# Attention's steps at fixed visits in a one-core encoder trunk

## The chip, the cores and the metric

The kernel runs on one core of a Trainium2 chip. The metric is the device time of one execution in microseconds (us). Five engines work side by side, each from its own queue and in that queue's order: TensorE (PE, matmuls; its weight loads are shown apart as PEld), VectorE (DVE), ScalarE (ACT), GpSimd (POOL) and SyncE (SP, which here issues transfers). Transfers run on 16 DMA engines. One engine waits for another through semaphores.

## The reference, cut to what matters

A trunk of two layers over 256 tokens of width 1024, all float32. A layer has a token mixer and a gated MLP, each behind an RMSNorm and with a residual sum. The mixer, cut to its core:

```python
u, q, k, v, g_pool, g_attn = split(xn @ w_in)
pool_out = (window means of u, four widths, minus u) @ w_pool * pool_scale
for g, (window, dilation) in enumerate(((128, 1), (512, 4), (2048, 16))):
    logits = q_g @ k_g * scale + bias_g           # +-64 keys, strided by the dilation
    o_g = softmax(logits) @ v_g ; lse_g = logsumexp(logits)
attn = sum over g of softmax_over_groups(lse)_g * o_g     # 4 heads of 128
merged = sigmoid(g_pool) * (pool_out @ w_a) + sigmoid(g_attn) * (attn @ w_b)
h = h + merged @ w_o
```

The weighted sum over the three groups equals one softmax over the keys of all three groups together, and that is how the kernel computes it: for each of the four heads and each half of the tokens one row of 512 logits (256 for group 0, 128 each for groups 1 and 2), one exponential, one division, and one sum of products with v over all of them.

## The kernel before, in words

Tokens are kept as two interleaved halves t = 0, 1 of 128. Nearly all matrix products are made with operands split into a high and a low part ("wh" and "wl" of weights, "xh" and "xl" of activations), so each weight tile that comes from memory as "raw" is cast to wh by ACT (line 177) and the rest made as wl by DVE (line 178). The class Weights does this in a fixed order of pieces given by `use`, up to three pieces ahead of the product that needs one; a 1 MB load into one of three raw buffers stands behind two pieces as a rule (`cols`: 256 columns, two pieces of 128). The load itself is line 117, on SP's queue.

`proj` (line 491 and 493) makes 128 output columns from one piece: eight matmuls with wh for 512 columns of x, eight with wl for 256. This is called a projection below. In a layer the mixer goes:

- values v of all twelve heads (lines 588, 757), then the pooling branch u, eight projections, and its window sums on DVE;
- q and k in six pairs of heads, PAIRS, four projections each (two heads of q, two of k). In the second pair (m == 1) a quarter of the pool products stands ahead of each projection (`pool_out`, matmuls at 483 to 485);
- eight projections of the pool branch with w_a into pa (`add_up`, 513 and 514), eight of the first gate, and then groups of the second gate and of w_b on attention's output at2.

Attention has four steps for each of the four heads hh:

- `scores` (881 to 908): for each t, matmuls of q and k into one bank (886, 891), bias added (897), negative maximum (902), exponential with its sum on ACT (905), reciprocal (907), scaling by it (908). It needs the head hh of all three groups, so heads 0 and 1 can go after the third pair and heads 2 and 3 after the sixth.
- `turn` (912 to 921): DVE transposes the probabilities in blocks of 32 x 32 into "rows" (915, one buffer, which shares its place with the norm's gain), and `cross` moves the sixteen blocks of 32 partitions to where a full transpose has them: sixteen transfers of 32 KB from "rows" to "pt" (598), on SP's queue. pt has one buffer.
- `parts` (923 to 931): pt's columns of group 0 split into high (pth, ACT, 929) and low (ptl, DVE, 930).
- `weigh` (933 to 949): six matmuls with split values (939) and eight with plain ones (943), the sum kept split in at2 (948, 949).

Before the change these steps stand in one list, two heads at a time: scores a, scores b, turn a, parts a, weigh a, turn b, parts b, weigh b. `step` takes the next one behind a projection: behind the second, third and fourth of the pairs m = 3, 4 and 5 until eight are done, and behind each of the eight projections into pa. The program is written in this order, and a planner, which has its own durations for each instruction, takes it as priorities: each engine's queue is filled with the first instruction in program order that is ready in the plan. So in the plan a weighting can come in the middle of a later projection, and the order on each engine is fixed when the kernel runs. Waits that come out longer than planned hold up everything behind them on that engine.

Of the kernel before, what the change touches and what calls it, by code (L numbers as in the profile page):

```python
# [10 lines left out]
F32 = mybir.dt.float32  # L11
# [5 lines left out]
P = 128  # L17
# [15 lines left out]
C_Q, C_K, C_V, C_GP, C_GA = 1024, 1024 + AW, 1024 + 2 * AW, 1024 + 3 * AW, 2048 + 3 * AW  # L33
# [3 lines left out]
WARM = (5, 1, 2, 1)  # L37
PAIRS = (2, 4, 0, 1, 3, 5)
LAG = 6
ENTRY = 4  # L40
HALVES = (slice(0, 512), slice(512, D))
SEGMENTS = (HALVES, (slice(0, 512), slice(512, 768), slice(768, D)))
# [162 lines left out]
def encoder(ctx, tc, x, w_in, w_pool, pool_scale, w_a, w_b, w_o, norm1, norm2, w_up, conv_w,  # L205
# [4 lines left out]
    big = ctx.enter_context(tc.tile_pool(name="big", bufs=1))  # L210
    sm = ctx.enter_context(tc.tile_pool(name="small", bufs=2))
# [5 lines left out]
    W = Weights(tc, wpool, big)  # L217

    def cols(w, c0):

        src = w[:, c0 : c0 + 256].rearrange("(k p) c -> p k c", p=P)
        return W.add(
            src, (8, 256), [((lambda t, j=j: t[:, :, j * P : (j + 1) * P]), (8, P)) for j in (0, 1)]
        )
# [10 lines left out]
    for l in range(DEPTH):  # L235
        for g in range(NG):
            c0 = C_V + g * 512
            slots = (("m2", 0, 2), ("m2", 1, 2), ("ybig",), ("at2",)) if g == 0 else ()
            for j in range(2):
                tag = "k1" if l == 0 and g == 1 and j == 0 else None  # L240
                W.use(rows(w_in[l], j * 512, 4, c0, 512, tag), slots[2 * j : 2 * j + 2])
        if l == 0:
            W.n_scaled = len(W.pieces)
        for c in range(3, -1, -1):
            W.use(cols(w_in[l], c * 256))
        for n, c in enumerate(PAIRS):
            pool = ([], [])
            if n == 1:
                pool = W.add(
                    w_pool[l].rearrange("g (k p) c -> p (g k) c", p=P), (8, 256),  # L250
                    [((lambda t, j=j: t[:, 4 * j : 4 * j + 4, :]), (4, 256)) for j in range(2)],
                )
                pool = (pool[:1], pool[1:])
            W.use(pool[0] + cols(w_in[l], C_Q + c * 256))
            W.use(pool[1] + cols(w_in[l], C_K + c * 256))
        for c in range(4):
            W.use(cols(w_a[l], c * 256))
        for c in range(4):
            W.use(cols(w_in[l], C_GP + c * 256))
        for c in range(2):  # L260
            W.use(cols(w_in[l], C_GA + c * 512))
            W.use(cols(w_in[l], C_GA + c * 512 + 256))
            src = w_b[l][:, c * 512 : (c + 1) * 512].rearrange("(k p) c -> p k c", p=P)
            W.use(
                W.add(
                    src, (4, 512),
                    [((lambda t, j=j: t[:, :, j * 256 : (j + 1) * 256]), (4, 256)) for j in (0, 1)],
                )
            )
        for c in range(4):  # L270
            W.use(rows(w_o[l], c * 256))
        slots = (("v1",), ("ybig",), ("at2",))
        for j in range(2):
            W.use(rows(w_up[l], j * 512, 4, 0, 512), slots[2 * j : 2 * j + 2])
        for f in range(0, NF, 2):
            a = cols(w_up[l], f * P) if f >= ENTRY else []
            g = cols(w_up[l], DFF + f * P)
            W.use([a[0], g[0], a[1], g[1]] if a else g)
            if f >= LAG:
                W.use(rows(w_down[l], (f - LAG) * P))  # L280
        for f in range(NF - LAG, NF, 2):
            W.use(rows(w_down[l], f * P))
# [5 lines left out]
    def gain(src):  # L288
        g = sm.tile([P, D], F32, tag="gain", bufs=1, name="gain")
        nc.sync.dma_start(out=g, in_=src.partition_broadcast(P))  # L290
        return g
# [203 lines left out]
    def proj(x2):  # L495

        i, (wh, wl) = W.get()
        ps = mmp.tile([P, 2, S], F32, tag="mm", name="proj_ps")
        two_sums(ps, lambda k: wh[:, k, :], lambda k: wl[:, k, :], x2, KD)
        W.free(i)  # L500
        return ps[:, 0], ps[:, 1]

    def halves(a):

        return a.rearrange("p (t m) -> p t m", t=2)
# [87 lines left out]
    def cross(out, in_):  # L593

        for i in range(4):
            for j in range(4):
                a, b = slice(32 * i, 32 * i + 32), slice(32 * j, 32 * j + 32)
                nc.sync.dma_start(out=out[b, i], in_=in_[a, j])  # L598

    def two_parts(tag, name):  # L600

# [163 lines left out]
    for l in range(DEPTH):  # L765
# [21 lines left out]
        if l == 0:  # L787
            with tc.manual_schedule():
                begun = begin_values_of_x()
            x2 = first_values(*begun, keep_values)  # L790
# [23 lines left out]
        for gi in range(3, -1, -1):  # L814
# [8 lines left out]
            cur, n = u, S + 2 * PAD  # L823
# [52 lines left out]
        q = big.tile([P, NH - HPG, 2, P], F32, tag="q1", name="q")  # L876
        kk = big.tile([P, NH - HPG, 2, P], F32, tag="k1", name="k")
        at2 = big.tile([P, HPG, 2, 2, P], F32R, tag="at2", name="at2")
        probs, ptiles = {}, {}

        def scores(hh):
            probs[hh] = sm.tile([P, 2, 512], F32, tag="s", name="probs")
# [29 lines left out]
        def turn(hh):  # L912

            rows = sm.tile([P, 4, 2, 4, 32], F32, tag="gain", bufs=1, name="rows")
            nc.vector.transpose(
                out=rows.rearrange("p j t c r -> p (t c) j r"),
                in_=probs[hh].rearrange("p t (c j r) -> p (t c) j r", c=4, j=4),
            )
            pt = sm.tile([P, 4, 2, 4, 32], F32, tag="pt", bufs=1, name="pt")
            cross(pt, rows)  # L920
            ptiles[hh] = pt

        def parts(hh):
            pt = ptiles[hh].rearrange("p i t c r -> p c t i r")
# [23 lines left out]
            nc.scalar.copy(out=oh, in_=ps)  # L948
            nc.vector.tensor_sub(out=ol, in0=ps, in1=oh.bitcast(F32))

        steps = []
        for a, b in ((0, 1), (2, 3)):
            steps += [(scores, a), (scores, b), (turn, a), (parts, a), (weigh, a)]
            steps += [(turn, b), (parts, b), (weigh, b)]

        def step():
            if steps:
                f, *which = steps.pop(0)
                f(*which)


        for m, c in enumerate(PAIRS):
            if m == 1:
                po2 = two_parts("m2", "po2")
                pool_parts = pool_out(po2)
            if m == 2:

                qkl = big.tile([P, 2, HPG, 2, P], F32R, tag="xn", name="qkl")
                ql, kl = qkl[:, 0], qkl[:, 1]
            for n in range(4):  # L970
                if m == 1:
                    next(pool_parts)
                src, rest = (halves(a) for a in proj(x2))
                hd = 2 * c + n % 2
                scale = HD**-0.5 if n < 2 else 1.0
                if hd < HPG:
                    hi, lo = ((qh, ql) if n < 2 else (kh, kl))
                    nc.scalar.mul(out=hi[:, hd], in_=src, mul=scale)
                    nc.vector.scalar_tensor_tensor(
                        out=lo[:, hd], in0=src, scalar=scale, in1=hi[:, hd].bitcast(F32),  # L980
                        op0=ALU.mult, op1=ALU.subtract,
                    )
                    nc.vector.scalar_tensor_tensor(
                        out=lo[:, hd], in0=rest, scalar=scale, in1=lo[:, hd].bitcast(F32),
                        op0=ALU.mult, op1=ALU.add,
                    )
                else:
                    o = (q if n < 2 else kk)[:, hd - HPG]
                    nc.scalar.mul(out=o, in_=rest, mul=scale)
                    nc.vector.scalar_tensor_tensor(  # L990
                        out=o, in0=src, scalar=scale, in1=o, op0=ALU.mult, op1=ALU.add
                    )
                if m >= 3 and n and len(steps) > 8:
                    step()

        pa = big.tile([P, KD, S], F32, tag="ybig", name="pa")
        for c in range(KD):
            add_up(pa[:, c, :], proj(po2))
            step()
        assert not steps  # L1000
        g2 = gain(norm2[l])


        gates = big.tile([P, 4, S], F32, tag="gates", name="gates")
# [7 lines left out]
        for c in range(KD):  # L1012
            th = gate(c)
            nc.vector.scalar_tensor_tensor(
                out=pa[:, c, :], in0=th, scalar=1.0, in1=pa[:, c, :], op0=ALU.add, op1=ALU.mult
            )
        m2 = big.tile([P, 2, KD, 2, P], F32R, tag="m2", name="m2")
        mh, ml = m2[:, 0], m2[:, 1]
        for c4 in range(2):
            ths = [gate(4 * c4 + j) for j in range(4)]  # L1020
            for j2 in range(2):
                i, (wh, wl) = W.get()
                for j in range(2):
                    c = 4 * c4 + 2 * j2 + j
# [3 lines left out]
                    m = sm.tile([P, S], F32, tag="u", name="m")  # L1028
# [5 lines left out]
                    m = halves(m)  # L1034
# [4 lines left out]
        x2 = two_parts("x", "x2")  # L1039
# [26 lines left out]

        a_first = big.tile([P, ENTRY, S], F32, tag="gates", name="a_first")

        rows_of_a = big.tile([P, 2, ENTRY * P], F32, tag="m2", name="a_rows")

# [5 lines left out]
        def turn_entry(t, r):  # L1076
            pt = mmp.tile([P, ENTRY, P], F32, tag="mm", name="a_turn")
            for f in range(ENTRY):
                nc.tensor.transpose(pt[:, f, :], r[:, f * P : (f + 1) * P], ident)
# [70 lines left out]
        for f in range(0, NF, 2):  # L1150
            up(f)
            up(f + 1)
            if f >= LAG:
                next(down)
                next(down)
        if l + 1 < DEPTH:
            x2 = two_parts("x", "x2")
# [34 lines left out]
```

## Time and profile before

| | us |
|---|---|
| median of 3 runs | 887.76 |
| the runs | 885.21, 887.76, 887.93 |
| profiled execution | 886.05 |
| its span, first to last instruction | 884.3 |
| PE busy in the span | 868.0 |
| DVE busy | 682.5 |
| ACT busy | 518.7 |

The granted clock of TensorE was 0.998 over the span. The page of the profile gives busy times, a chain of waits followed back from the last instruction, and the costliest groups. Views of the trace behind it answer more: the waits (who waited for whom), the timeline (instructions in order of time; neighbours of one kind merged, with "x16" for sixteen), and tables of busy time by stretch. In layer 0 attention's steps run from about 106 to 191 us, in layer 1 from about 544 to 626 us. A merged line of SP for `cross` gives the time that SP's queue took to issue the sixteen transfers.

### The profile page before, as it was taken

How to read it: one execution, taken by the hardware profiler on the slowest of the kernel's cores; microseconds unless marked ns; L12 is line 12 of the kernel's file. 1: busy time of each engine (PE TensorE's matmuls, PEld its weight loads, DVE VectorE, ACT ScalarE, POOL GpSimd, SP SyncE). 2: the span in 40 equal slices, each digit the busy share in tenths (PEclk: the TensorE clock that was granted, in tenths of full speed). 3: DMA queues.
4: the chain of work that ended last, by engine and by line, in shares of the span. 5: the costliest groups of instructions: out<-in, count | busy, mean ns of one | idle time of the engine just before them, and what ended most of it. 6: DMA issues, size and time to landing. Idle time of an engine off the chain costs nothing.

```text
span 884.3 us, 12920 instructions
## 1 busy us (share of the span) xinstructions
PE 868.0 (98%) x4778; PEld 752.8 (85%) x4778; DVE 682.5 (77%) x1150; ACT 518.7 (59%) x905; POOL 14.7 (2%) x45
## 2 busy tenths in 40 slices
PE   9999999999999999999999999999999999999997
PEld 7888887888888888888888898888888888888886
DVE  6997785857869987787756977776678698878774
ACT  6755553556648766666545564554566486656653
POOL 2000000000000000000000000000000000000000
PEclk9999999999999999999999999999999999999999
DMA  9669636466564665565626465544755447556541
GB/s 326 214 232 297 226 117 196 157 222 208 179 207 146 208 219 191 165 215 191 238 96 237 144 215 168 170 164 135 269 188 191 158 155 247 182 191 199 182 143 49
DMA packets 132236, 168.86 MB, mean 191 GB/s; under 512 B 5302, under 2 KB 112518, under 8 KB 132044
## 3 DMA queue, kind: packets, MB, share of 16 engines
q1 hardware_dynamic: 132156, 168.02, 57.0%
q8 instruction: 38, 0.62, 0.3%
q14 instruction: 26, 0.21, 0.1%
q10 hardware_dynamic: 16, 0.00, 0.0%
HBM read 162.74 MB, written 3.69 MB: 188 GB/s over the span
## 4 chain that ended last, share of the span: by engine, by line
PE 82%; SPq 8%; DMA 3%; DVE 3%; issue 1%; ACT 1%; ACTq 0%; POOLq 0%; POOL 0%; DVEq 0%
PE proj_ps L491 30%; PE proj_ps L493 16%; SPq L598 8%; PE res_ps L518 6%; PE v_ps L588 6%; PE res_ps L519 6%; PE res_ps L520 6%; PE v_ps L757 2%; PE b_ps L491 2%; DMA pt<-rows 2%; PE v_ps L670 1%; DMA raw<-in_w_in_dram 1%; PE o_ps L939 1%; PE o_ps L943 1%; PE b_ps L493 1%
## 5 line engine op out<-in xcount | busy, mean ns | idle before, releaser
L178 DVE TENSOR_TENSOR wl<-raw,wh 128x1024 fp32r<-128x1024 f32 x274 | 333.8, 1223 | 121.5 <-ACT wh L177 119.6
L177 ACT CAST wh<-raw 128x1024 fp32r<-128x1024 f32 x274 | 286.1, 1049 | 183.0 <-PE proj_ps L491 113.6
L491 PE MATMUL proj_ps<-x,wh 128*128 128x512 f32 x1408 | 353.2, 392 | 0.0
L491 PEld LDWEIGHTS proj_ps<-x,wh 128*128 128x128 f32 x1408 | 254.1, 189 | 46.0
L493 PEld LDWEIGHTS proj_ps<-x,wl 128*128 128x128 f32 x1408 | 192.5, 190 | 13.8
L493 PE MATMUL proj_ps<-x,wl 128*128 128x256 f32 x1408 | 197.6, 282 | 0.0
L518 PE MATMUL res_ps<-wh,actq 128*128 128x512 f32 (+1 forms) x184 | 70.2, 381 | 0.0
L519 PE MATMUL res_ps<-wl,actq 128*128 128x512 f32 (+1 forms) x184 | 70.1, 381 | 0.0
L520 PE MATMUL res_ps<-wh,actk 128*128 128x512 f32 (+1 forms) x184 | 69.9, 380 | 0.0
L520 PEld LDWEIGHTS res_ps<-wh,actk 128*128 128x128 f32 x184 | 34.6, 188 | 6.7
L518 PEld LDWEIGHTS res_ps<-wh,actq 128*128 128x128 f32 x184 | 34.7, 188 | 6.2
L519 PEld LDWEIGHTS res_ps<-wl,actq 128*128 128x128 f32 x184 | 34.7, 188 | 6.0
L491 PE MATMUL proj_ps<-po,wh 128*128 128x512 f32 x128 | 33.6, 396 | 0.0
L1122 ACT ACTIVATE y<-y 128x256 f32<-128x256 f32 x44 | 18.3, 416 | 24.4 <-DVE y L1119 24.2
L1105 ACT ACTIVATE y<-a,prm 128x256 f32<-128x256 f32 x36 | 21.6, 599 | 16.1 <-DVE a L514 16.1
L425 ACT ACTIVATE junk<-h 128x512 f32<-128x512 f32 (+1 forms) x20 | 10.9, 547 | 27.7 <-DVE h L423 27.7
L518 PE MATMUL res_ps<-wh,m 128*128 128x512 f32 (+1 forms) x72 | 26.5, 368 | 0.0
L519 PE MATMUL res_ps<-wl,m 128*128 128x512 f32 (+1 forms) x72 | 26.3, 366 | 0.0
L520 PE MATMUL res_ps<-wh,m 128*128 128x512 f32 (+1 forms) x72 | 26.3, 365 | 0.0
L491 PEld LDWEIGHTS proj_ps<-po,wh 128*128 128x128 f32 x128 | 22.7, 189 | 3.7
L588 PE MATMUL v_ps<-wh,x 128*128 128x512 f32 x80 | 25.7, 392 | 0.0
L1106 DVE SCALAR_TENSOR_TENSOR y<-a,prm,y 128x255 f32<-128x255 f32 x36 | 17.3, 481 | 8.1 <-ACT y L1105 8.1
(205 smaller groups left out, 1094.6 us busy)
## 6 DMA issues: line engine op xcount, KB each, us to landing
raw<-in_w_in_dram SPq DMA_DIRECT2D x58, 1024.0 KB
raw<-in_w_up_dram SPq DMA_DIRECT2D x44, 1024.0 KB
raw<-in_w_down_dram SPq DMA_DIRECT2D x22, 1024.0 KB
raw<-in_w_a_dram SPq DMA_DIRECT2D x8, 1024.0 KB
raw<-in_w_o_dram SPq DMA_DIRECT2D x8, 1024.0 KB
pt<-rows SPq DMA_DIRECT2D x128, 32.0 KB
raw<-in_w_b_dram SPq DMA_DIRECT2D x4, 1024.0 KB
sk<-fd SPq DMA_DIRECT2D x1, 2560.0 KB
```

Source lines behind the costliest of these rows:

```text
L177: lambda: nc.scalar.copy(out=h, in_=src),
L178: lambda: nc.vector.tensor_sub(out=l, in0=src, in1=h.bitcast(F32)),
L491: nc.tensor.matmul(ps, wh(k), x2[:, k], start=(k == 0), stop=False)
L493: nc.tensor.matmul(ps[:, 1], wl(k), x2[:, k, 0], start=False, stop=(k == nk - 1))
L518: nc.tensor.matmul(ps, ah, wh, start=first, stop=False)
L519: nc.tensor.matmul(ps, ah, wl, start=False, stop=False)
L520: nc.tensor.matmul(ps, al, wh, start=False, stop=last)
L588: nc.tensor.matmul(ps, x2[:, 2 * n + j, part, t, :], w[:, j, :], start=(n + m == 0), stop=(n == 3 and m == 5),)
L598: nc.sync.dma_start(out=out[b, i], in_=in_[a, j])
L757: nc.tensor.matmul(ps[t], a[:, k, t, :], w[:, j, :], start=(k + m == 0), stop=(k == KD - 1 and m == 2),)
L1105: nc.scalar.activation(y, a, AF.Identity, bias=b, scale=w1)
L1122: nc.scalar.activation(y2, y2, AF.Tanh, scale=c)
```

## The change

The places behind which a step can go are now called visits and counted from 0 to 27: the four projections of each pair m = 3, 4, 5 (0 to 11), the eight into pa (12 to 19) and the eight of the first gate (20 to 27). A table gives each step of each head its visit. Heads 0 and 1: scores at 0 and 3, turn at 1 and 5, parts at 6 and 10, weigh at 7 and 11. Heads 2 and 3: scores at 12 and 13, turn at 13 and 17, parts at 18 and 22, weigh at 19 and 23. `cross` becomes a generator that issues four transfers and pauses; each visit, after its steps, lets the oldest unfinished one go on. So a head's transfers stand in the program at four visits, from its turn's visit on for heads 0 and 2, and from the one after for heads 1 and 3, since the visit of their turn ends the one before.

pt is now one tile for two heads, in the place "ybig" for heads 0 and 1 (between plh, the pooled branch, and pa) and in the place "xn" for heads 2 and 3 (after qkl, the low parts of q and k). "rows" keeps its one buffer. Therefore the load of the second norm's gain, which has the same place as "rows", moves from before the gates to after the first gate. In the second pair each quarter of the pool products stands behind its projection and not ahead of it, and the pool weights' pieces stand between the two pieces of a column block.

```diff
+VISITS = ((0, 3, 12, 13), (1, 5, 13, 17), (6, 10, 18, 22), (7, 11, 19, 23))
...
-            W.use(pool[0] + cols(w_in[l], C_Q + c * 256))
-            W.use(pool[1] + cols(w_in[l], C_K + c * 256))
+            for j, c0 in enumerate((C_Q, C_K)):
+                a, b = cols(w_in[l], c0 + c * 256)
+                W.use([a] + pool[j] + [b])
...
             for j in range(4):
                 a, b = slice(32 * i, 32 * i + 32), slice(32 * j, 32 * j + 32)
                 nc.sync.dma_start(out=out[b, i], in_=in_[a, j])
+            yield
...
-        probs, ptiles = {}, {}
+        probs, ptiles, crossing = {}, {}, []
...
-            pt = sm.tile([P, 4, 2, 4, 32], F32, tag="pt", bufs=1, name="pt")
-            cross(pt, rows)
-            ptiles[hh] = pt
+            if hh % 2 == 0:
+                ptiles["pair"] = big.tile(
+                    [P, 2, 4, 2, 4, 32], F32, tag=("ybig", "xn")[hh // 2], name="pt"
+                )
+            ptiles[hh] = ptiles["pair"][:, hh % 2]
+            crossing.append(cross(ptiles[hh], rows))
...
-        steps = []
-        for a, b in ((0, 1), (2, 3)):
-            steps += [(scores, a), (scores, b), (turn, a), (parts, a), (weigh, a)]
-            steps += [(turn, b), (parts, b), (weigh, b)]
+        visits = [[] for _ in range(28)]
+        for f, at in zip((scores, turn, parts, weigh), VISITS):
+            for hh, visit in enumerate(at):
+                visits[visit].append((f, hh))
 
         def step():
-            if steps:
-                f, *which = steps.pop(0)
-                f(*which)
+            for f, hh in visits.pop(0):
+                f(hh)
+            if crossing and next(crossing[0], "end") == "end":
+                crossing.pop(0)
...
             for n in range(4):
+                src, rest = (halves(a) for a in proj(x2))
                 if m == 1:
                     next(pool_parts)
-                src, rest = (halves(a) for a in proj(x2))
...
-                if m >= 3 and n and len(steps) > 8:
+                if m >= 3:
                     step()
...
-        assert not steps
-        g2 = gain(norm2[l])
...
             nc.vector.scalar_tensor_tensor(
                 out=pa[:, c, :], in0=th, scalar=1.0, in1=pa[:, c, :], op0=ALU.add, op1=ALU.mult
             )
+            step()
+        assert not any(visits) and not crossing
+        g2 = gain(norm2[l])
```

## The prediction

> **What bounds the kernel now.** I read the page first, then the waits, then a table by stretch for the two stretches in which attention's steps run, then the timeline there. The page:
>
> ```profile
> span 884.3 us, 12920 instructions
> PE 868.0 (98%) x4778; PEld 752.8 (85%) x4778; DVE 682.5 (77%) x1150; ACT 518.7 (59%) x905; POOL 14.7 (2%) x45
> PE 82%; SPq 8%; DMA 3%; DVE 3%; issue 1%; ACT 1%; ACTq 0%; POOLq 0%; POOL 0%; DVEq 0%
> ```
>
> TensorE (PE) is busy but for 884.3 - 868.0 = 16.3 us. The chain of waits gives SyncE's queue (SPq) 8%, but it only follows one path back: while SPq issues, PE has projections to do. What SPq costs is PE's own idle time, and the waits say what ends it:
>
> ```profile
> PE o_ps L939 <- ACT pth L929: 8.3, 7, 1.9
> ...
> ACT pth L929 <- DMA pt<-rows: 16.0, 8, 3.3
> ...
> DVE rows L915 <- DMA pt<-rows: 9.0, 4, 2.7
> ```
>
> Columns: total us, times, longest. PE waits 8.3 us in seven of eight heads for the split (pth) of the turned probabilities; the split waits for the transfers. The table by stretch (start:end, length, then busy us of each engine) shows that this is all the idle time there:
>
> ```profile
> 105.70:191.23 85.53, 81.74 (x497) 72.00 (x497) 60.64 (x100) 40.80 (x77) 0.00 (x0) 1.00 0.49 159
> 543.84:625.68 81.84, 77.22 (x474) 67.99 (x472) 56.99 (x96) 38.99 (x72) 0.00 (x0) 1.00 0.48 154
> ```
>
> 85.53 - 81.74 = 3.8 us in layer 0 and 81.84 - 77.22 = 4.6 us in layer 1, together the 8.3 (rounded). The clock was 1.00 in both. The change can win this, and little else.
>
> One pair of heads in the timeline (start, length, engine, line, tiles; idle time before it in brackets):
>
> ```profile
> 111.12 0.28 PE L886 MATMUL s_ps<-kh,qh 128*128 128x256 f32 x1
> ...
> 115.53 0.28 PE L886 MATMUL s_ps<-kh,qh 128*128 128x256 f32 x1
> ...
> 118.28 0.42 DVE L983 SCALAR_TENSOR_TENSOR qkl<-proj_ps,qkl 128x256 fp32r<-128x256 f32 x1
> 118.62 1.28 DVE L897 TENSOR_TENSOR probs<-s_ps,bt 128x512 f32<-128x512 f32 x2
> ...
> 119.94 2.00 PE L491 MATMUL proj_ps<-x,wh 128*128 128x512 f32 x8
> ...
> 121.54 1.23 DVE L915 STREAM_TRANSPOSE rows<-probs 128x1024 f32<-128x1024 f32 x1
> ...
> 122.73 2.00 PE L491 MATMUL proj_ps<-x,wh 128*128 128x512 f32 x8
> 122.79 10.91 SPq L598 DMA_DIRECT2D pt<-rows  x16
> ...
> 133.80 1.14 SPq L117 DMA_DIRECT2D raw<-in_w_a_dram  x2
> ...
> 135.47 0.38 PE L939 MATMUL o_ps<-pth,vh 128*128 128x256 f32 x1 [1.89 <-ACT pth L929]
> ...
> 138.63 10.02 SPq L598 DMA_DIRECT2D pt<-rows  x16
> ...
> 150.61 0.39 PE L939 MATMUL o_ps<-pth,vh 128*128 128x256 f32 x1
> ...
> 161.28 10.01 SPq L598 DMA_DIRECT2D pt<-rows  x16
> ...
> 172.86 1.25 DVE L915 STREAM_TRANSPOSE rows<-probs 128x1024 f32<-128x1024 f32 x1 [2.73 <-DMA pt<-rows]
> ...
> 176.39 10.44 SPq L598 DMA_DIRECT2D pt<-rows  x16
> ...
> 556.49 10.02 SPq L598 DMA_DIRECT2D pt<-rows  x16
> ...
> 571.74 10.86 SPq L598 DMA_DIRECT2D pt<-rows  x16
> ...
> 595.18 10.01 SPq L598 DMA_DIRECT2D pt<-rows  x16
> ...
> 610.16 11.06 SPq L598 DMA_DIRECT2D pt<-rows  x16
> ```
>
> Read from it: a projection takes 122.73 - 119.94 = 2.79 us of PE. Sixteen transfers take 10.0 us of SPq at best and 83.33 / 8 = 10.4 on average, so 0.4 us of lateness per block that comes and goes, up to 1.05. From the end of a block (138.63 + 10.02) to the weighting at 150.61: 1.96 us of landing and split. From the end of a block (161.28 + 10.01) to the end of the next head's transpose (172.86 + 1.25): 2.8. Two weight loads cost SPq 1.14, 0.57 each. From here on a block is 10.02 us and its in-block load 0.57.
>
> **The change, part by part.**
>
> *Later weighting.* It adds no work: eight heads, 128 transfers, the same matmuls. It sets how much PE work stands between a head's scores and its weighting, and what else is in the way. The price of the PE work itself:
>
> ```profile
> 111.29 0.36 PE s_ps L886 x3
> 111.65 0.45 PE s_ps L891 x4
> ...
> 137.03 0.58 PE o_ps L939 x5
> 137.62 0.99 PE o_ps L943 x8
> ```
>
> Scores of a head: 2 x (0.36 + 0.45) = 1.62 us. Weighting: 0.58 + 0.99 and a first matmul of some 0.12, 1.7.
>
> Let s be the first matmul of scores 0. After the change PE has, before weighting 0 (visit 7): two heads' scores and seven projections, 3.24 + 7 x 2.79 = 22.8 us. Weighting 1 (visit 11) comes 1.7 + 4 x 2.79 later, at s + 35.65. The second pair (scores at visits 12 and 13, weightings at 19 and 23) has the same two distances from its own s.
>
> What must be done by then. Head 0: in the rows above the softmax chain of the first head and the eviction of the next visit end where the other head's work begins, at 118.62, 7.5 us after 111.12. Scores 1 now comes three visits later, so the transpose can go there: s + 7.5 + 1.25 = 8.8. Then a block and a load, 10.59, and 1.96: s + 21.35. Slack 1.4 us, 1.0 with the average slow issue. No stall.
>
> Head 1: "rows" is still one buffer, so its transpose waits until head 0's transfers have landed: 8.8 + 10.59 + 2.8 = 22.2. A second block, load and split: s + 34.75, against 35.65. Slack 0.9, or 0.1 with two average slow issues; with two of the slowest (2.1) it is 1.2 short. I take a stall of 0.3.
>
> Head 2: turn 2 is in the same visit as scores 3 and behind it. Bounds for its transpose: 8.8 as above, and 11.65 as in the first pair now (121.54 + 1.23 - 111.12). Nearest is the second pair of layer 0 now, where the scores of head 3 began at 155.45 and this transpose was next:
>
> ```profile
> 155.45 0.28 PE L886 MATMUL s_ps<-kh,qh 128*128 128x256 f32 x1
> ...
> 159.91 1.24 DVE L915 STREAM_TRANSPOSE rows<-probs 128x1024 f32<-128x1024 f32 x1
> ```
>
> So 5.7 us after scores 3, which comes 1.62 + 2.79 = 4.4 after scores 2: 10.1. Then 10.1 + 10.59 + 1.96 + 0.4 = 23.05 against 22.8: a stall of 0.25, between none and 1.8.
>
> Head 3: 10.1 + 13.39 + 10.59 + 1.96 + 0.8 = 36.85, against 35.65 + 0.25: a stall of 0.95, between none and 2.3 when head 2 was as late as its bound.
>
> Sum of what is left: (0 + 0.3 + 0.25 + 0.95) x 2 layers = 3.0 us, of 8.3. The bounds are 0 and (1.2 + 1.8 + 2.3) x 2 = 10.6.
>
> *Buffers.* A head's transfers need not wait for the weighting before it to let go of pt (now the second block starts at 138.63, as the weighting ends, 3.6 us after the landing). What they wait for next is the transpose, 2.8 us after the block. That is in the sum. The pair in "ybig" holds back pa's first eviction until weighting 1 is done, but PE does weighting 1 before that projection: nothing. The pair in "xn" waits for qkl's last reader, scores 3, over long before transpose 2: nothing.
>
> *Transfers four per visit.* In program order a visit's four transfers now stand behind that visit's weight load. Four take 2.5 us of a 2.79 us visit and a load comes every second visit, so one load falls into each block: the 0.57 above. Behind a transfer on SPq stand only weight loads. They were held up by a whole block until now (133.80 is right at the end of one) and no PE wait names a projection, so weights arriving earlier wins nothing. If instead a load has to wait for its raw buffer, the transfers behind it wait too:
>
> ```profile
> SPq L117 <- DVE qkl L979: 13.1, 2, 7.6
> ```
>
> That is the one place where SPq itself could lose: two such waits of 13.1 us in this stretch. I take 0, because SPq runs some two visits behind the program in a block and the buffer should be free by then; what a wait costs is in the rivals.
>
> *Pool parts behind the projection, their weights between the column pieces.* One visit's projection moves ahead of a pool part:
>
> ```profile
> 74.50 1.05 ACT L177 CAST wh<-raw 128x1024 fp32r<-128x1024 f32 x1 [2.56 <-DMA raw<-in_w_in_dram]
> ...
> 76.94 0.28 PE L483 MATMUL pool_ps<-plh,wh 128*128 128x256 f32 x1
> 77.46 0.39 PE L484 MATMUL pool_ps<-pll,wh 128*128 128x256 f32 x1 [0.24 <-DVE pll L849]
> ...
> 78.87 2.00 PE L491 MATMUL proj_ps<-x,wh 128*128 128x512 f32 x8
> ```
>
> In layer 0 the first of them would start when the pool part does now, at 76.94 and not at 78.87. Its weights' cast is the one that waited for its load, 74.50 + 1.05 = 75.55: cover 1.4 us, and what a load is late beyond that would be a stall. The 0.24 us wait for pll goes. I take a gain of 0.2.
>
> *gain(norm2) after the gates.* It is read here first:
>
> ```profile
> L450 DVE SCALAR_TENSOR_TENSOR xn<-h,rstd,gain x24: 475/480/486, 254.8 to 696.6; 128x256 f32<-128x256 f32 x24
> ```
>
> That is at 254.8 us; the last of eight gates after 191.2 ends at 191.2 + 8 x 2.79 = 213.5. 41 us stay for one load. Nothing.
>
> Sum: -8.3 + 3.0 - 0.2 = -5.5 us. The profiled execution took 886.05 us (span 884.3), the median of three is 887.76, the lowest 885.21. I go from the mean of these four, 886.7: **881 us**.
>
> [...] The loads that stood behind a block now stand inside it, and share the DMA engines with it:
>
> ```profile
> 135.00:141.40 6.40, 1.00 1.02 342
> ```
>
> Two loads issued from 133.80 filled all DMA engines from 135.0 to 141.4: 3.2 us each, from 1.2 us after the issue. No block of before had a load this close ahead of its last transfer. [...]
>
> **The rivals.** One formula prices a delay d in every block: per layer the stalls add up to 2d - 0.1 for the first pair (slack 0.1) and 2d + 1.2 for the second, 4d + 1.1. It breaks even with 8.5 us at d = 0.8.
>
> 1. All stalls go: the softmax chains end early, slow issues miss the blocks. 886.7 - 8.5 = 878. For it: slacks of 1.4 and 0.9 without slow issues. Against: head 3.
> 2. The stalls only move, to heads 1 and 3, since the blocks are still in series through "rows": upper bounds, -8.5 + 10.6, 889; half way there 885.5 to 887, no change.
> 3. A load waits on SPq for its raw buffer and holds the transfers behind it (slower). With d = 2 us: 2 x 9.1 - 8.5 = +9.7, 896. It is slower by 0.3% (2.7 us, about what a measurement of this kernel can tell) from d = 1.1. For it: the row with 7.6 us. Against: those loads were not behind ten microseconds of transfers.
> [...]
>
> **How the numbers follow.** The forecast has 0.42, the first rival 0.23, the second 0.15, the third 0.12, the fourth 0.08. Faster: 0.23 and nearly nine tenths of the forecast's, 0.37, together 0.60. Same: the rest of the forecast and most of the second, 0.18. Slower: 0.22. The range runs from 877.5, all stalls gone, to 889, the upper bounds; beyond it lie the third and fourth rival. The likeliest case has 879 to 884.
>
> **What would show it.** Right: PE's wait for pth at 3 us or less, in weightings 1 and 3 first; blocks of 16 transfers with a load among them; the two stretches some 80 and 78 us for the same instructions. Wrong: a wait of SPq's weight loads between the transfers, landings more than 2 us after a block's end, PE waits for proj weights, or the planner placing a weighting where its tile is not ready.

## The result, and the profile after

The changed kernel is slower: 891.94 us (median of 9 runs, 890.10 to 895.86) against 885.28 us for the kernel before (9 runs, 884.38 to 887.93), a ratio of 1.0079 with an interval of 1.0065 to 1.0092. The profiled execution took 890.26 us, its span 888.5 us against 884.3. So the traces tell of 4.2 us, and the medians lie 6.7 apart: of the nine executions the profiled one is the second fastest, and most of the slower ones had a lower granted clock (down to 0.989, against 0.995 here), but no trace shows where they lost it. The page of the changed kernel:

```profile
span 888.5 us, 12913 instructions
PE 869.5 (98%) x4778; PEld 754.9 (85%) x4778; DVE 682.6 (77%) x1150; ACT 518.5 (58%) x905; POOL 15.5 (2%) x45
PE 83%; DMA 7%; SPq 4%; DVE 2%; ACT 1%; issue 1%; POOLq 0%; DVEq 0%; ACTq 0%; POOL 0%
```

PE's idle time grew from 16.3 to 888.5 - 869.5 = 19.0 us, and its busy time for the same 4778 matmuls by 1.5 us. In the chain the SyncE queue's share fell from 8% to 4%, as meant, and that of the DMAs rose from 3% to 7%. The waits of the changed kernel (total us, times, longest):

```profile
ACT wh L178 <- DMA raw<-in_w_in_dram: 18.6, 7, 4.2
...
PE o_ps L945 <- ACT pth L935: 7.1, 4, 3.6
...
ACT gates L515 <- PE o_ps L945: 5.0, 2, 2.5
PE o_ps L945 <- DVE ptl L936: 3.6, 6, 0.9
```

And the first and the third of them in the kernel before:

```profile
ACT wh L177 <- DMA raw<-in_w_in_dram: 11.5, 5, 2.9
...
ACT gates L513 <- PE o_ps L939: 2.2, 2, 1.1
```

PE's stalls at the weightings are 7.1 + 3.6 = 10.7 us, where 8.3 stood before and 3.0 were forecast. ACT now waits for weight loads for 18.6 us, 7.1 more. Where the stalls are, the timeline of PE in the changed kernel shows, layer 0 and then layer 1 (idle time in brackets):

```profile
145.50 0.39 PE L945 MATMUL o_ps<-pth,vh 128*128 128x256 f32 x1 [0.46 <-ACT pth L935]
146.85 0.39 PE L945 MATMUL o_ps<-ptl,vh 128*128 128x256 f32 x1 [0.27 <-DVE ptl L936]
173.04 0.39 PE L945 MATMUL o_ps<-ptl,vh 128*128 128x256 f32 x1 [0.68 <-DVE ptl L936]
188.76 0.39 PE L945 MATMUL o_ps<-pth,vh 128*128 128x256 f32 x1 [2.65 <-ACT pth L935]
190.05 0.58 PE L945 MATMUL o_ps<-ptl,vh 128*128 128x256 f32 x1 [0.90 <-DVE ptl L936]
...
581.50 0.38 PE L945 MATMUL o_ps<-pth,vh 128*128 128x256 f32 x1 [0.32 <-ACT pth L935]
582.85 0.38 PE L945 MATMUL o_ps<-ptl,vh 128*128 128x256 f32 x1 [0.27 <-DVE ptl L936]
608.90 0.39 PE L945 MATMUL o_ps<-ptl,vh 128*128 128x256 f32 x1 [0.55 <-DVE ptl L936]
625.65 0.38 PE L945 MATMUL o_ps<-pth,vh 128*128 128x256 f32 x1 [3.65 <-ACT pth L935]
626.94 0.58 PE L945 MATMUL o_ps<-ptl,vh 128*128 128x256 f32 x1 [0.91 <-DVE ptl L936]
```

Head 0 never stalls, heads 1 and 2 by 0.55 to 0.73 us, and head 3 by 2.65 + 0.90 = 3.55 us in layer 0 and 4.56 us in layer 1. The table by stretch puts a price on that. Each stretch runs from the first score matmul of head 2 to the first product with w_b (start:end, length, then busy us of PE, PEld, DVE, ACT, POOL, the granted clock, DMA share, GB/s). Before:

```profile
150.83:213.41 62.58, 60.81 (x369) 53.62 (x368) 42.84 (x72) 32.85 (x63) 0.00 (x0) 1.00 0.62 208
584.70:664.81 80.11, 77.69 (x465) 68.34 (x464) 57.13 (x98) 44.45 (x86) 0.00 (x0) 1.00 0.60 203
```

After, with two short stretches right behind head 3's stalls ahead of them:

```profile
189.53:192.94 3.41, 2.89 (x14) 2.89 (x14) 1.82 (x6) 1.42 (x6) 0.00 (x0) 0.50 1.06 415
626.43:629.85 3.42, 2.91 (x14) 2.91 (x14) 1.82 (x6) 1.44 (x6) 0.00 (x0) 0.50 1.07 419
149.30:215.33 66.03, 61.80 (x362) 54.68 (x361) 43.39 (x71) 32.77 (x62) 0.00 (x0) 0.97 0.51 168
585.29:669.02 83.73, 78.63 (x458) 69.46 (x457) 57.68 (x97) 44.30 (x85) 0.00 (x0) 0.98 0.52 170
```

The second pair's stretches are 3.45 and 3.62 us longer: 2.46 and 2.68 us more idle time of PE, and 0.99 and 0.94 us more busy time, because TensorE's granted clock was 0.50 for 3.41 us right behind each of head 3's stalls. The stretches don't hold quite the same work: the one before also has 13 of the 14 matmuls of weighting 1 in it, 7 matmuls more in all (x369 against x362), so the loss in the second pair, and the gain elsewhere, are somewhat larger than these differences (an estimate: 0.3 us in each layer). All the rest of the kernel, the first pair of heads above all, became 3.45 + 3.62 - 4.2 = 2.9 us shorter. So the change won in the first pairs and lost 7.1 us in the second ones.

How head 3 of layer 0 comes to stall, in the timeline of the changed kernel (SyncE's queue, then ACT and DVE, then PE):

```profile
172.38 2.41 SPq L600 DMA_DIRECT2D pt<-rows  x4
174.88 1.69 SPq L118 DMA_DIRECT2D raw<-in_w_in_dram  x1
176.62 5.23 SPq L600 DMA_DIRECT2D pt<-rows  x8
181.96 0.52 SPq L118 DMA_DIRECT2D raw<-in_w_in_dram  x1
182.52 2.48 SPq L600 DMA_DIRECT2D pt<-rows  x4
...
187.99 0.34 SPq L292 DMA_DIRECT2D gain<-in_norm_dram  x1
...
181.43 2.03 ACT L178 CAST wh<-raw 128x1024 fp32r<-128x1024 f32 x2 [3.51 <-DMA raw<-in_w_in_dram]
187.36 1.04 ACT L178 CAST wh<-raw 128x1024 fp32r<-128x1024 f32 x1 [3.90 <-DMA raw<-in_w_in_dram]
188.31 0.71 ACT L935 CAST pth<-pt 128x256 fp32r<-128x256 f32 x2
188.43 1.23 DVE L179 TENSOR_TENSOR wl<-raw,wh 128x1024 fp32r<-128x1024 f32 x1 [3.56 <-ACT wh L178]
189.57 0.75 DVE L936 TENSOR_TENSOR ptl<-pt,pth 128x256 fp32r<-128x256 f32 x2
...
185.00 1.11 PE L495 MATMUL proj_ps<-x,wl 128*128 128x256 f32 x8
```

Two weight loads stand inside the block. The second is issued at 181.96, and behind it the last four transfers, the last of them at 184.42. A transfer or a load has landed when the last of its completion signals is in the trace. The load landed at 187.26, the four transfers right behind it, the last at 187.97, 3.55 us after its issue. (The load of the gain, which needs the place of "rows", goes out at 187.99.) In a block without a load inside, the last transfer landed 1.83 to 1.89 us after its issue: so in all eight blocks of the kernel before, and in those of heads 0 and 2 here. The blocks of heads 1 and 3, which have a load with four transfers behind it, took 3.55 to 3.88.

On ACT, head 3's split (pth) stands behind the cast of that load's weights, which waits until 187.36 and ends at 188.40, and on DVE its low part (ptl) behind the low part of the weights. The split starts at 188.31, 0.34 us behind the landing. PE had finished the fourth projection of the first gate at 186.11 and waited. In layer 1 the block lands at 624.87, 3.63 us after its last issue, and the split starts at 625.20. In the kernel before, layer 0's block 3 began 4.0 us later (176.39), and its split started at 188.18 all the same. PE came to the weighting there at 188.22, 2.1 us later than here: what the first pair had won was waited for again.

### The profile page after: what moved, and what is told of

It reads as the page before. It is cut to its first block, busy times and chain, and to the rows that moved or that the text cites. A ratio compares the mean times of both kernels' runs of the same rounds, so it can differ in the third digit from the quotient of the medians.

```text
span 888.5 us, 12913 instructions
## 1 busy us (share of the span) xinstructions
PE 869.5 (98%) x4778; PEld 754.9 (85%) x4778; DVE 682.6 (77%) x1150; ACT 518.5 (58%) x905; POOL 15.5 (2%) x45
## 4 chain that ended last, share of the span: by engine, by line
PE 83%; DMA 7%; SPq 4%; DVE 2%; ACT 1%; issue 1%; POOLq 0%; DVEq 0%; ACTq 0%; POOL 0%
PE proj_ps L493 31%; PE proj_ps L495 16%; PE res_ps L520 6%; PE v_ps L590 6%; PE res_ps L521 6%; PE res_ps L522 6%; SPq L600 4%; DMA raw<-in_w_in_dram 4%; PE v_ps L760 2%; DMA raw<-in_w_a_dram 2%; PE b_ps L493 2%; DMA sk<-fd 1%; PE v_ps L673 1%; ACT wh L178 1%; PE b_ps L495 1%; PE o_ps L949 1%
```

## The experiments

Theory A, on which the first four runs rest: the time is lost because weight loads stand between the fours of block 3, and later or whole blocks would win it back. Its rivals, which the expectations name by letters, put the loss elsewhere: in the new order of the pool's products, in the half clock, or in something that keeps the stall wherever the steps stand.

**e1_block.** All sixteen transfers at the visit of the turn.

```diff
                 nc.sync.dma_start(out=out[b, i], in_=in_[a, j])
-            yield
+        yield
```

> The changed kernel with all sixteen transfers of a head issued at the visit of its turn again; visits and buffers stay. Theory A (the weight loads between the transfers make the fourth head's weighting late: three weight casts that wait for such loads stand ahead of its split on ScalarE, and the transfers themselves end later): the wait before the fourth weighting, 2.65 + 0.90 us in layer 0 and 3.65 + 0.91 us in layer 1 of the changed kernel, falls under 1 us, no stretch of half clock is left near 190 and 627 us, 878 to 882 us. Rival B (the blocks stay in series through one buffer of rows, so later visits only move the waits): the wait before the fourth weighting stays above 2 us and the time at 888 or more.

Measured: 891.4 us, ratio to before 1.0072 (1.0057 to 1.0087). PE's waits, and the timeline of SyncE's queue, ACT and PE around head 3:

```profile
PE proj_ps L493 <- DVE gates L516: 9.3, 2, 4.9
PE o_ps L945 <- DVE ptl L936: 1.7, 2, 1.2
```

```profile
172.12 11.16 SPq L600 DMA_DIRECT2D pt<-rows  x16
183.37 2.65 SPq L118 DMA_DIRECT2D raw<-in_w_in_dram  x3
...
184.71 0.71 ACT L935 CAST pth<-pt 128x256 fp32r<-128x256 f32 x2 [7.02 <-DMA pt<-rows]
188.63 1.99 ACT L178 CAST wh<-raw 128x1024 fp32r<-128x1024 f32 x2 [3.21 <-DMA raw<-in_w_in_dram]
...
192.46 3.78 PE L493 MATMUL proj_ps<-x,wh 128*128 128x512 f32 x8 [4.94 <-DVE gates L516]
```

Half of theory A holds: with no load in the block, its last transfer landed 1.84 us after its issue, the split starts 184.71 - (172.12 + 11.16) = 1.43 us behind the block's end, and weighting 3 waits for nothing. But nothing is won, where 878 to 882 us were expected. The loads come behind the block, ACT's cast waits for them, the sums of the first gate stand behind that cast, and now the fifth gate projection waits, 4.94 us in layer 0 and 9.3 in all. Something lets the gate projections run only four ahead.

**e2_late_split.** Head 3's split and weighting at visits 24 and 25, transfers by fours.

```diff
-VISITS = ((0, 3, 12, 13), (1, 5, 13, 17), (6, 10, 18, 22), (7, 11, 19, 23))
+VISITS = ((0, 3, 12, 13), (1, 5, 13, 17), (6, 10, 18, 24), (7, 11, 19, 25))
```

> The changed kernel with the fourth head's split and weighting two visits later (24 and 25 for 22 and 23), transfers four per visit as in the change. Theory A: the data comes some 3.5 to 4.5 us late, two visits are 5.6 us, so the wait before the fourth weighting goes, with it the half clock, and 878 to 883 us are left, although the loads still stand between the transfers. Rival C (the loads between the transfers starve the projections themselves): projections wait for weights and the time stays above 887.

Measured: 891.9 us, ratio 1.0079 (1.0062 to 1.0096), where 878 to 883 were expected. The stall is there as in the changed kernel (timeline of PE):

```profile
190.24 0.38 PE L945 MATMUL o_ps<-pth,vh 128*128 128x256 f32 x1 [2.35 <-ACT pth L935]
191.53 0.56 PE L945 MATMUL o_ps<-ptl,vh 128*128 128x256 f32 x1 [0.90 <-DVE ptl L936]
```

The order of PE's matmuls did not change: weighting 3 still stands right behind the fourth gate projection, two visits ahead of where the program has it. The reason is in the code. The weighting reads vl, and the gate sums are written to the same place:

```python
mmp = ctx.enter_context(tc.tile_pool(name="mmp", bufs=4, space=bass.MemoryType.PSUM))
...
vl = big.tile([P, 2, 512], F32R, tag="gates", name="vl")
...
gates = big.tile([P, 4, S], F32, tag="gates", name="gates")
```

No gate sum can be evicted before the last weighting has read vl, so four gate projections fill the four banks and the fifth has to wait. This is theory P, formed here, and the row "ACT gates L515 <- PE o_ps L945" of the changed kernel, 5.0 us in two waits, is its trace. The kernel before has the same wait, with 2.2 us. Weighting 3 has a latest place that no visit moves.

**e3_pool_back.** The pool's products ahead of their projections and the pool weights in the old order.

```diff
-                src, rest = (halves(a) for a in proj(x2))
                 if m == 1:
                     next(pool_parts)
+                src, rest = (halves(a) for a in proj(x2))
...
-            for j, c0 in enumerate((C_Q, C_K)):
-                a, b = cols(w_in[l], c0 + c * 256)
-                W.use([a] + pool[j] + [b])
+            W.use(pool[0] + cols(w_in[l], C_Q + c * 256))
+            W.use(pool[1] + cols(w_in[l], C_K + c * 256))
```

> The changed kernel with the order of the pool parts and of the pool weights as before the change. Theory A: the 0.5 us wait of a pool part for DVE in layer 0 goes and nothing else, at most 1 us, so about 890 to 892 us. Rival D (the new order of weight pieces delays all loads behind it): back to 886 or less.

Measured: 890.98 us, ratio 1.0066 (1.0050 to 1.0083). The interval overlaps that of the changed kernel. The pool's order isn't what made it slower.

**e4_filler.** 24 added matmuls ahead of head 3's weighting, into the bank that the weighting then overwrites, so that PE is busy where it stalled.

```diff
             ps = acc.tile([P, 2, P], F32, tag="acc", name="o_ps")
+            if hh == 3:
+                for _ in range(24):
+                    nc.tensor.matmul(
+                        ps, at2[:, 0, 0, 0, :], at2[:, 0, 0], start=True, stop=True
+                    )
```

> The changed kernel with 24 more matmuls of 256 columns (some 2.8 us of PE) right ahead of the fourth head's weighting in each layer, into the bank that the weighting then overwrites. Nothing is left out. Theory E (PE's idle 3.5 to 4.5 us there are what brings the half clock of 3.4 us behind it): PE is never idle for more than 1.8 us there, the half clock at 190 and 627 us goes, and the kernel is 1 to 3 us faster than the changed one although it does more, 888 to 890 us median with less scatter. If the half clock has another cause: the half clock stays, and the time is that of the changed kernel or up to 1 us above it.

Measured: 891.06 us (887.44 to 891.89), ratio 1.0060 (1.0037 to 1.0083). In the profiled execution, the one of 887.44 us, the clock stayed at 1.00 behind head 3 (1.00 from 186 to 195 us and from 622 to 631), and the span was 885.7, 2.8 us below the changed kernel's. The three other executions took 890.26 to 891.89 with a granted clock of 0.997. So here the half clock goes with the long stall: the nine executions of the changed kernel have 0.995 at most. What the three lost stays open, since no trace shows them; as a price of the half clock, this run is inconclusive.

The next four runs test theory P. The old pt buffer left 4 KB per partition free, which is what gates needs.

**f1_gates_place.** gates in a place of its own, nothing else.

```diff
-        gates = big.tile([P, 4, S], F32, tag="gates", name="gates")
+        gates = big.tile([P, 4, S], F32, tag="gown", name="gates")
```

> The changed kernel, but the tile gates has a place of its own and no longer that of vl; nothing else differs. Theory P (place): weighting 3 reads vl, the gate sums write the same place, so the first four gate projections keep all four PSUM banks until weighting 3 has read vl, and PE can't pass it: its stall of 2.65 + 0.90 us (layer 0) and 3.65 + 0.91 us (layer 1) sits on the end. With an own place PE goes on, weighting 3 comes two projections later, both stalls go under 0.5 us, TensorE isn't half-clocked behind them (1.2 to 1.7 us each in the changed kernel): 890 - 8.1 - 2.9 + 1 = 880 (878 to 884). Rival L (loads): the weights' loads that stand between block 3's transfers are late anyway, and the projections wait for their weights as long: 887 to 892, with PE waiting at proj_ps instead of o_ps.

Measured: 882.2 us (9 runs), ratio 0.9967 (0.9948 to 0.9985). That is 9.7 us below the changed kernel, for one name. PE's waits, head 3's first matmul, and the second pair's stretches in the table:

```profile
PE o_ps L945 <- DVE ptl L936: 1.8, 4, 0.7
PE o_ps L945 <- ACT pth L935: 1.2, 3, 0.8
```

```profile
190.79 0.38 PE L945 MATMUL o_ps<-pth,vh 128*128 128x256 f32 x1 [0.77 <-ACT pth L935]
```

```profile
149.70:211.74 62.04, 60.58 (x363) 53.12 (x362) 43.59 (x71) 32.99 (x62) 0.00 (x0) 1.00 0.54 179
581.62:659.15 77.53, 76.99 (x458) 67.87 (x457) 58.15 (x97) 44.71 (x85) 0.00 (x0) 1.00 0.55 184
```

Weighting 3 now stands inside the sixth gate projection. Its stall is 0.77 us in layer 0 (0.5 was expected at most) and none in layer 1. The stretches are 3.99 and 6.20 us shorter than in the changed kernel: 2.77 and 4.56 us of PE's idle time, and 1.22 and 1.64 us of busy time, most of it what the half clock had cost (2.9 us of busy time at 0.50 can cost 1.5 at most, an estimate). No wait on weights took the stalls' place, so rival L (late loads) falls.

**f2_place_and_later** (f1 and e2 together) and **f3_place_later_block** (with e1 as well).

> As f1_gates_place, and head 3's split and weighting two visits later in the program (24 and 25 for 22 and 23). Theory P: now the visits count, weighting 3 stands one projection later than in f1_gates_place and waits for nothing (under 0.2 us): the time of f1_gates_place or up to 1 us less (878 to 883). Rival L: 887 to 892.

> As f2_place_and_later, with all sixteen transfers at the visit of the turn, as before the change. If the spreading by four costs something of its own (a load between a block's fours delays the block, a block's fours delay a load), this differs from f2_place_and_later by over 1 us; theory P says that either order of the queue is hidden once PE can pass weighting 3: within 1 us of f2_place_and_later. Rival L: with the block whole, the loads come still later, PE waits at proj_ps as with e1_block: 888 to 892.

Measured: f2 881.09 us, ratio 0.9949 (0.9935 to 0.9964); f3 877.56 us, ratio 0.9910 (0.9896 to 0.9925). f2 is as theory P expects, but for a wait of 0.39 us at weighting 3 of layer 1 (under 0.2 was expected). f3 isn't: it was to lie within 1 us of f2 and lies 3.5 us below. With whole blocks PE's stalls at weightings 1 are gone and only these are left, for heads 2:

```profile
PE o_ps L945 <- DVE ptl L936: 1.2, 2, 0.7
```

So spreading by fours has a price of its own, which shows only once gates doesn't hide it: 0.5 us between the changed kernel and e1_block, 3.5 us here. In f2 the last transfers of the blocks of heads 1 and 3 land 3.59 to 4.23 us after their issue, behind a load, in f3 1.83 to 1.88. The two profiled executions have spans of 879.2 and 875.0 us. PE's stalls at the weightings are 1.3 us of these 4.2 (2.1 + 0.4 in f2 against 1.2), and 2.2 are busy time (866.8 against 864.6 us); what makes the busy time isn't settled.

**f4_place_all_later.** gates in its own place, weightings 1, 2 and 3 one, one and two visits later, the pool's order as before the change, transfers by fours.

```diff
-VISITS = ((0, 3, 12, 13), (1, 5, 13, 17), (6, 10, 18, 22), (7, 11, 19, 23))
+VISITS = ((0, 3, 12, 13), (1, 5, 13, 17), (6, 11, 19, 24), (7, 12, 20, 25))
```

> The tile gates in its own place, weighting 1, 2 and 3 one, one and two visits later (12, 20, 25), their splits 11, 19, 24, and the second pair's pool products and weights in the order of before the change. Theory P: no stall over 0.3 us is left at any weighting; against f2_place_and_later the stalls of heads 1 and 2 (0.7 us each and layer) go as well: 876 to 881. If their stalls only move (the split stands behind other work on ACT and DVE), the same as f2_place_and_later within 1 us. Rival L: 886 to 892.

Measured: 874.61 us, ratio 0.9881 (0.9864 to 0.9897), below what was expected, and with g1 the fastest of all. PE's list of waits in its profile names no weighting any more; these are its two longest:

```profile
PE gain_ps L334 <- DVE ones L320: 1.0, 1, 1.0
PE pool_ps L485 <- DVE pll L851: 0.5, 1, 0.5
```

**g1_all_later_block** (f4 with whole blocks) and **g2_block_pool_back** (f3 with the pool's old order).

> f4_place_all_later with each head's sixteen transfers at the visit of its turn. Theory S (spreading by four costs 3.5 us, f2 to f3, because a load between the fours delays a block that is waited for): in f4_place_all_later no weighting waits any more, so there is nothing left for the block to save: 873.5 to 875.7, within 1 us of it. Rival L: whole blocks delay the loads by up to 11 us, and without slack at the weightings PE now waits at proj_ps: 876 to 882. Rival M (the four's price is not the wait but the extra breaks in a projection's matmuls): 871 to 873.

> f3_place_later_block (gates in its own place, head 3 two visits later, whole blocks) with the second pair's pool products and weights in the order of before. The wait of 1.5 us at the pool products and the later first scores are what is at stake. Theory: 1 to 2 us less than f3_place_later_block, 875.5 to 876.7. If the order of the pool products is worth nothing behind the wait: 877 to 878.5. If it is the order, and not the later weightings, that makes most of the 6.5 us from f2_place_and_later to f4_place_all_later: 873 to 874.5.

Measured: g1 874.44 us, ratio 0.9879 (0.9864 to 0.9894); g2 876.18 us, ratio 0.9899 (0.9884 to 0.9913). In f4 the last transfers of heads 1 and 3 still land 3.57 to 3.83 us after their issue, in g1 1.83 to 1.85: whole blocks win nothing where no weighting waits, as theory S says. With the stalls out of the way the old order of the pool's products is worth 1.4 us by the medians (f3 to g2), within its expectation, though the intervals of the two ratios still overlap.

**g3_before_place** and **g4_before_pair.** The kernel before, its steps untouched, with pt for two heads (g4), and with gates in its own place besides (g3).

```diff
-            pt = sm.tile([P, 4, 2, 4, 32], F32, tag="pt", bufs=1, name="pt")
-            cross(pt, rows)
-            ptiles[hh] = pt
+            if hh % 2 == 0:
+                ptiles["pair"] = big.tile(
+                    [P, 2, 4, 2, 4, 32], F32, tag=("ybig", "xn")[hh // 2], name="pt"
+                )
+            ptiles[hh] = ptiles["pair"][:, hh % 2]
+            cross(ptiles[hh], rows)
```

> The kernel before, with pt as a tile for two heads in the places ybig and xn (as the change has it) and, in the room so won, a place of its own for gates; steps, transfers and pool as before. Theory P: of the 8.3 us of stalls before, only those of weighting 3 (0.41 and 1.24 us) hang on the place, and the pairs let block b start without a wait for pt: 880 to 885. Rival V (the place alone makes the gain, the visits nothing): 874 to 879.

> The kernel before with pt for two heads as the change has it, and nothing else: gates stays in the place of vl. It shows what the large buffers do by themselves. Theory P: the turn of the second head of a pair no longer waits for the first one's weighting, so block 3 starts earlier, and weighting 3 keeps its place behind the fourth gate projection: its stall goes or stays under 1.3 us, the others stay: 882 to 887. Rival B (the large buffers' places, xn with qkl and ybig with plh, hold the turns back): 888 to 894.

Measured: g3 886.02 us, ratio 1.0007 (0.9998 to 1.0016), outside its 880 to 885; g4 886.69 us, ratio 1.0015 (1.0005 to 1.0024), within its 882 to 887. With the old steps neither the large buffers nor the place win anything: in g3 weighting 3 no longer waits, but 7.2 us of stalls are left at the others, and two of these, of 1.78 and 2.28 us, have the half clock behind them (0.50 for 3.41 us each). The change alone loses 6.7 us, the place with the large buffers wins nothing by itself, and both together win 3.6 us (f1) and, with later visits and the pool's old order, 11 (f4).

## Why the prediction was wrong

It said 881.0 us, faster, and the kernel took 891.94, outside the range of 877.5 to 889. By its own steps:

- *Heads 0, 1 and 2.* Forecast stalls per layer 0, 0.3 and 0.25; measured 0, 0.73 and 0.59 for the two layers' heads 1, and 0.68 and 0.55 for heads 2. That the sizes came within 0.3 to 0.4 us is partly luck. Head 1 of layer 0 took 145.50 - (138.82 + 2.49) = 4.19 us from the end of its block to the weighting, not 1.96, since its last transfer landed behind a load; but PE, which does this weighting in the middle of a projection, came there at 145.04, 1.5 us later than the sum has it. The stall of heads 2 is that of the low part alone, which stands on DVE behind head 3's transpose and has no term. The first pairs had 8.3 - 1.77 - 2.42 = 4.1 us of stalls, of which the forecast left 0.6; measured, all but the second pairs' stretches won 2.9 us.
- *Head 3.* This is the step that failed: "a stall of 0.95, between none and 2.3" against 3.55 and 4.56. Its sum has the split ready at s + 36.85. With s = 149.30 for layer 0 that is 186.15, and the weighting began at 188.76, 2.61 later. Two of its terms were too small. The block took 185.00 - 172.38 = 12.62 us with two loads in it, one of which took 1.69 us to issue, not 10.59 + 0.4 with one. And from the end of the block to the weighting it took 3.76 us, not 1.96: the last transfer landed 3.55 us after its issue, behind the load inside the block, and not 1.84. The ACT cast ahead of the split was over 0.43 us after the landing; in e1_block the split began 0.18 us after it, so the cast cost some 0.2 us (an estimate). Block 3 began 0.41 us ahead of the forecast, and the 0.4 us of slow issue given to block 2 wasn't needed: 1.63 + 1.80 - 0.81 = 2.62. PE came to the weighting 0.91 us later than forecast (186.11, not s + 35.9), so the stall was 0.95 + 2.61 - 0.91 = 2.65. The low part on DVE, behind the low part of that load's weights, added 0.90, which has no term at all.
- *"One load falls into each block"*: the blocks of heads 0 and 2 hold none, those of heads 1 one, those of heads 3 two.
- "*No PE wait names a projection, so weights arriving earlier wins nothing*" costed the moved loads at nothing, by PE's waits alone. With a load among them, the last transfers of the blocks landed 3.55 to 3.88 us after their issue, not 1.83 to 1.89, and ACT and DVE take a weight's cast and a head's split in the order of the plan. e1_block shows the same from its other side: the loads behind the block, and PE waits for the gates.
- *"Later weighting adds no work."* True, but the prediction took the visit for the place. Weighting 3 can't go behind the fifth gate projection as long as gates has vl's place (e2_late_split, f1_gates_place). That bound is in both kernels; the prediction has no term for what the gates' sums wait for, though the kernel before shows the wait (2.2 us, in the section on the result).
- *The clock* had no term. "The clock was 1.00 in both" was read as a constant. Behind head 3's stalls it was 0.50 for 3.41 us in each layer: some 0.9 to 1.5 us each, by the two comparisons and the estimate above.
- *The pool's order*: 0.2 us were forecast as gained. e3_pool_back leaves it open, g2_block_pool_back has it as a loss of 1.4 us by the medians.
- *The rivals.* The second, stalls that only move to heads 1 and 3 (889 us at its upper bounds), is nearest in time, at 0.15. Of the third, only the slow load issue inside the block is there (1.69 us against 0.52), not a d of 2 us in every block. The fourth, at 0.08, transfers that wait behind a load, is nearest in kind. Before the result that was an assumption, shown by no run; in the changed kernel two blocks of four in each layer have it, with last transfers that landed 3.55 to 3.88 us after their issue. It was thought to cost nothing where four transfers stand behind the load, since by the two loads of 133.80 a load should land 4.4 us after its issue (1.2 + 3.2, an estimate). The load issued at 181.96 took 5.30, and the four transfers landed 0.2 to 0.7 us behind it, some 1.7 us late. The load isn't held up in turn: ACT got the one with four transfers behind it 187.36 - 181.96 = 5.40 us after its issue, and in e1_block the one with only loads behind it 188.63 - 183.37 = 5.26.

The miss in the profiled executions: 4.2 us more span where 5.5 less were forecast, 9.7 in all. The stalls make 10.7 - 3.0 = 7.7 of it, the busy time 1.5 (1.9 more in the second pairs' stretches, a little less elsewhere), and 0.5 is other idle time, among it the 0.2 that the pool's order was to win.

## What to carry to other kernels

A step's latest place is set by who is waiting for its buffers, not only by where the program calls it: before counting slack, look for the tile that shares the place of one of its operands, and for how many banks the next writers may fill meanwhile. When transfers on a queue are spread, count what a load between them does to those behind it, and what they do to a load behind all of them: here the transfers behind a load landed 1.7 to 2.0 us later (3.55 to 3.88 us after their issue for 1.83 to 1.89), and the late loads of e1_block had PE wait 9.3 us for the gates. ACT and DVE, which take both in one order, passed the delay on although no wait of PE had named a projection. Where a change removes stalls of 1 to 2 us, ask what longer stall it may leave: here 3.55 us at one weighting and the half clock behind it (0.50 for 3.41 us) cost layer 0 more than its three of 1.89, 1.36 and 0.41 us had.

## What the runs showed of the hardware

In the kernel before and in the changed one the last transfer of a block landed 1.83 to 1.89 us after its issue in all twelve blocks without a load inside, and 3.55 to 3.88 us in the four that have a 1 MB load with four transfers behind it on the same queue.

PE's stalls had half clock behind them in several runs. In the changed kernel stalls of 2.65 and 3.65 us were each followed by 3.41 us at a granted clock of 0.50. In e1_block the half clock began within the stalls of 4.94 and 4.38 us, 1.69 and 0.93 us before their end, and lasted twice as long:

```profile
190.77:197.59 6.82, 5.13 (x16) 4.36 (x17) 5.43 (x12) 4.44 (x11) 0.00 (x0) 0.50 1.04 364
627.68:634.50 6.82, 5.89 (x18) 5.02 (x19) 4.67 (x11) 4.04 (x9) 0.00 (x0) 0.50 0.95 330
```

In g3_before_place half clock follows a shorter stall, of 1.78 us.

```profile
135.06 0.39 PE L942 MATMUL o_ps<-pth,vh 128*128 128x256 f32 x1 [1.78 <-ACT pth L932]
```

```profile
136.32:139.73 3.41, 3.41 (x16) 3.30 (x15) 1.69 (x3) 0.39 (x2) 0.00 (x0) 0.50 0.60 204
```

PE is busy throughout these 3.41 us, so the clock cost about half of them, 1.7 us (an estimate), as much as the stall.

In the kernel before it doesn't follow one of 1.89 us (at 135.47; the clock was 1.00 from 130 to 145 us), nor in g4_before_pair one of 1.77 us (at 583.20; 1.00 from 582.5 to 586). So the length of a stall alone didn't tell whether half clock followed; what did isn't settled.

The nine runs of the changed kernel also spread along the clock: 890.10 us at a mean of 0.995, 895.86 us at 0.989.
